# Half of the low parts of the block inputs subtracted by GpSimd, in six matmul stages of a hybrid decoder block

## The chip, the cores and the metric

The kernel runs on one core of a Trainium2 chip. The metric is the device time of one execution in microseconds (us); lower is better. Engines are called by the profile's names: PE is TensorE (PEld its weight loads), DVE is VectorE, ACT is ScalarE, POOL is GpSimd, SP is SyncE, which issues most loads.

## The reference

One decoder block over 2048 tokens of width 1024, in float32:

```python
u = rmsnorm(h, norm_mix_g); z = u @ w_in            # 1024 -> q, k, v, pz, ga, gp
a = dilated window attention(q, k, v); p = multi-scale pooling(pz)
merged = sigmoid(ga) * (a @ w_att_out) + sigmoid(gp) * (p @ w_pool_out)
h = h + merged @ w_out
m = rmsnorm(h, norm_mlp_g)
h = h + square(relu(m @ w_mlp_in)) @ w_mlp_out
return rmsnorm(h, norm_final_g)
```

## The kernel before

**Products.** A float32 product is made of three matmuls in a rounded type. `split` (L138 to L145) makes two tiles of a source tile of 128 x 512: `hi`, the rounded copy, cast by ACT (L143), and `lo` = source minus `hi`, subtracted by DVE (L144). `mm_acc` then issues three matmuls for each pair of blocks: hi times hi (L150), lo of one with hi of the other (L151), and hi with lo (L152).

**Stages.** The big projections run in a scheme of the Strassen kind: a 2 x 2 block product takes seven combined products. `stage` walks over pairs of rows of the weight, two pairs at a time; in each of the seven steps of `ORDER1` it splits the weight's combination (tiles `wh`, `wl`) and multiplies it with the input's combination (tiles `mB11h`/`mB11l`, `mT1h`/`mT1l` and so on, four tiles k = 0 to 3 each). The seven input combinations are made once for a stage, by `make` in `combine`, during its first two pairs: B11, T1, T2, B22, T3, B21, T4. The T ones are subtractions done in place (L203, L207, L212, L217): T1 overwrites the buffer that B11 was split from, T2 that of T1. So the next subtraction on a buffer has to wait until the split has read it. All input tiles stay until the stage ends.

There are six such stages: the mixer projections of the first and of the second half of the tokens (tiles with `u`; with buffer numbers `u0`, `u1`), the output projection of either half (`o0`, `o1`), and the first MLP product of either half (`c0`, `c1`). Below they are called A to F in this order. The second MLP product (L699 on) has its own splits (`xh`, `xl`) and is not touched.

**Order.** The program is put in order by a scheduler that lists instructions by its own timeline; each engine then runs its list strictly in order, waiting on semaphores. POOL's list holds no arithmetic in the stages: it issues the DMAs that write results to DRAM (`sg_d`, `mg_d`, `h_d`, `hg_d`, `hid_d`, `w2s_d`). Raw weights (`r_c` and the like) come in by SP into four buffers, so a load waits until the last use of the buffer. `w2_sums` (L691) makes the sums s1 to s4 of a second weight as a hook between pairs, out of the same four raw buffers.

Of the kernel before, what the change touches and what calls it, by code (L numbers as in the profile page):

```python
# [9 lines left out]
F32 = mybir.dt.float32  # L10
# [37 lines left out]
def trunk_kernel(ctx: ExitStack, tc, xt, w_qk, w_v, w_pz, w_grp, w_gates, w_att, w_pool, w_o, w_1, w_2, cols, out):  # L48
    nc = tc.nc
# [68 lines left out]
    def pool_of(stack, name, **kw):  # L118
        return stack.enter_context(tc.tile_pool(name=name, bufs=1, reuse_waits="tile", **kw))
# [15 lines left out]
        nc.vector.tensor_scalar(t, t, -0.5, 1.5, op0=ALU.mult, op1=ALU.add)  # L135
        nc.vector.tensor_mul(dst, y, t)

    def split(pool, src, key, tag, bufs):  # L138

        n = src.shape[-1]  # L140
        hi = pool.tile([P, C], F32R, name=f"{tag}h_{key}", tag=tag + "h", bufs=bufs)[:, :n]
        lo = pool.tile([P, C], F32R, name=f"{tag}l_{key}", tag=tag + "l", bufs=bufs)[:, :n]
        nc.scalar.copy(hi, src)  # L143
        nc.vector.tensor_sub(lo, src, hi.bitcast(F32))  # L144
        return hi, lo  # L145

    def mm_acc(ps, terms, start, stop):
# [25 lines left out]
    KH = KD // 2  # L173
    wps = ExitStack()
    wp = pool_of(wps, "wp")
# [14 lines left out]
    def combine(piece, key):  # L190


        b11, b12, b22, b21 = ({} for _ in range(4))

        def make(name):
            out = []
            for k in range(KH):
                if name == "B11":
                    x = b11[k] = piece(k, 0, "tt")
                elif name == "T1":  # L200
                    b12[k] = piece(k, 1, "hx")
                    x = b11[k]
                    nc.vector.tensor_sub(x, b12[k], x)  # L203
                elif name == "T2":
                    b22[k] = piece(k + KH, 1, "h22")
                    x = b11[k]
                    nc.vector.tensor_sub(x, b22[k], x)  # L207
                elif name == "B22":
                    x = b22[k]
                elif name == "T3":  # L210
                    x = b22[k]
                    nc.vector.tensor_sub(x, x, b12[k])  # L212
                elif name == "B21":
                    x = b21[k] = piece(k + KH, 0, "hx")
                else:
                    x = b11[k]
                    nc.vector.tensor_sub(x, b21[k], x)  # L217
                out.append(split(wp, x, f"{key}_{k}", "m" + name, KH))
            return out
        return make  # L220

# [76 lines left out]
    def stage(pairs, make, hook=None):  # L298
# [4 lines left out]
        for j0 in range(0, len(pairs), 2):  # L303
# [6 lines left out]
            for n, step in enumerate(ORDER1):  # L310
                a, b, bk = step.split()
                if j0 == 0:
                    m[b] = make(b)
                for key, _, scale, onto, fin in js:
                    wh, wl = split(wp, w[key][a], f"{key}_{a}", "w", WB)
                    first = n in (0, 1, 5)
                    if first:
                        bank[key, bk] = bank_of(bk, f"{key}_{bk}{n}")
                    ps = bank[key, bk]
                    mm_acc(ps, [(wh[:, k * P:(k + 1) * P], wl[:, k * P:(k + 1) * P], *m[b][k])  # L320
                                for k in range(KH)], first, True)
                    if n in (0, 1, 2):
                        row, t = ((0, 0), (1, 1), (0, 1))[n]
                        x = mid[key, n] = wtile(f"z{a}_{key}")
                        if onto:
                            nc.sync.dma_start(x, onto(row, t))
                            nc.vector.tensor_add(x, ps, x)
                        else:
                            total(x, ps, None, scale and scale[row])
                    elif n < 6:  # L330
                        fin(*{3: (0, 1), 4: (1, 1), 5: (0, 0)}[n], ps, mid[key, {3: 2, 4: 1, 5: 0}[n]])
                    else:
                        fin(1, 0, ps, None)
# [230 lines left out]
    def merge(hf):  # L564
# [4 lines left out]
        for t in range(2):  # L569
            c = 2 * hf + t  # L570
            for n in range(6):
                x = temp(f"p_{c}_{n}", "hx")
                nc.sync.dma_start(x, p_d[c, n])
                pa[t, n] = split(wp, x, f"pa_{c}_{n}", next(tags), KH)
# [315 lines left out]
```

## Time and profile before

| | |
|---|---|
| median of 3 runs | 2850.49 us (2848.96 to 2852.53) |
| the profiled execution, its own time | 2848.74 us |
| span of its instructions | 2847.0 us |
| PE busy | 2639.0 us, 93% |
| DVE busy | 1817.7 us, 64% |
| ACT busy | 1365.9 us, 48% |
| POOL busy | 581.7 us, 20% |
| mean granted PE clock | 0.958 |

PE is the engine that is busy nearly all the time; what counts is where it is not. Shares over the whole span are means over stages that differ much, so the rows below are taken by stretches.

### The profile page before, as it was taken

Reading aid. Unit: us, or ns where it says so; the run is one execution under the profiler, and the core shown is the slowest. Engines: PE = TensorE matmul, PEld = TensorE weight load, DVE = VectorE, ACT = ScalarE, POOL = GpSimd, SP = SyncE. Lnnn points to the kernel's source line nnn. Section 1 sums busy time; section 2 is a strip of 40 time slices with the busy share of each in tenths; the row PEclk is TensorE's granted clock in tenths of the full one; section 3 lists DMA queues with packets and bytes.
Section 4 is the critical chain, followed back from the end, with each engine's and each line's share of the span. In section 5 each row is a group of like instructions: output and inputs, shape, how many; then the busy total and the mean of one; then the engine's idle time right before and its main releaser. Section 6 shows DMA issues by size and latency. Waiting matters only on the chain.

```text
span 2847.0 us, 35963 instructions
## 1 busy us (share of the span) xinstructions
PE 2639.0 (93%) x11866; PEld 2079.0 (73%) x11866; DVE 1817.7 (64%) x3009; ACT 1365.9 (48%) x2659; POOL 581.7 (20%) x1003
## 2 busy tenths in 40 slices
PE   6999999899989996778888999989998999999996
PEld 5777777677757774556676888878887788878885
DVE  4745546854645565857888656766555585688457
ACT  5444444544444443233555555655555544564444
POOL 2134421124453342221121221122211000000000
PEclk8999999899979998898999999999999999999998
DMA  6334444244344347797675554455546746673434
GB/s 187 126 101 136 136 130 139 94 113 137 129 136 136 122 162 172 232 248 230 220 252 214 192 184 173 155 176 192 183 166 244 257 146 187 228 234 113 136 101 129
DMA packets 204650, 480.29 MB, mean 169 GB/s; under 512 B 41440, under 2 KB 44992, under 8 KB 204464
## 3 DMA queue, kind: packets, MB, share of 16 engines
q1 hardware_dynamic: 131984, 290.07, 31.8%
q0 software_dynamic: 72480, 187.93, 20.2%
q8 instruction: 94, 1.54, 0.2%
q14 instruction: 92, 0.75, 0.1%
HBM read 326.65 MB, written 151.14 MB: 168 GB/s over the span
## 4 chain that ended last, share of the span: by engine, by line
PE 72%; DMA 9%; DVE 8%; issue 7%; ACT 2%; POOL 2%; SPq 0%; DVEq 0%; POOLq 0%; ACTq 0%
PE z L152 7%; PE z L151 7%; PE z L150 6%; PE z_c_b L150 4%; PE z_c_b L152 4%; PE z_c_b L151 4%; PE z_c_c L152 3%; PE z_c_c L150 3%; PE z_c_c L151 3%; PE s L441 2%; PE z_g_b L150 2%; PE z_g_b L152 2%; PE z_g_b L151 2%; PE o L457 1%; PE z_g_c L151 1%
## 5 line engine op out<-in xcount | busy, mean ns | idle before, releaser
L144 DVE TENSOR_TENSOR wl_S<-r_S,wh_S 128x512 fp32r<-128x512 f32 x128 | 88.5, 692 | 123.6 <-ACT wh_S L143 123.6
L143 ACT CAST wh_S<-r_S 128x512 fp32r<-128x512 f32 x128 | 79.8, 624 | 175.6 <-PE z L151 157.4
L144 DVE TENSOR_TENSOR wl_c_S<-s_c,wh_c_S 128x512 fp32r<-128x512 f32 x128 | 87.9, 689 | 100.8 <-ACT wh_c_S L143 100.6
L151 PE MATMUL z<-xl_T,wh_S 128*128 128x512 f32 x384 | 149.6, 390 | 2.8 <-DVE xl_T L144 2.8
L152 PE MATMUL z<-xh_T,wl_S 128*128 128x512 f32 x384 | 149.4, 389 | 0.0
L150 PE MATMUL z<-xh_T,wh_S 128*128 128x512 f32 x384 | 138.7, 389 | 0.0
L760 POOL TENSOR_TENSOR y<-y,frs 128x256 f32<-128x256 f32 x4 | 3.2, 813 | 659.8 <-ACT fsq L745 652.2
L447 ACT ACTIVATE sb<-sb,negm 128x256 f32<-128x256 f32 (+1 forms) x192 | 87.3, 456 | 102.5 <-DVE negm L445 102.4
L143 ACT CAST wh_c_S<-s_c 128x512 fp32r<-128x512 f32 x128 | 77.6, 619 | 102.9 <-PE z_c_b L151 49.2
L443 DVE SCALAR_TENSOR_TENSOR sb<-steps,s 128x256 f32<-128x256 f32 (+1 forms) x192 | 63.7, 360 | 97.5 <-PE s L441 97.0
L144 DVE TENSOR_TENSOR wl_A<-r_A,wh_A 128x512 fp32r<-128x512 f32 x96 | 66.0, 689 | 67.3 <-ACT wh_A L143 51.1
L696 POOL DMA_DIRECT2D w2s_d<-s_w x64 | 34.6, 541 | 359.9 <-DVE s_w L275 326.1
L143 ACT CAST wh_A<-r_A 128x512 fp32r<-128x512 f32 x96 | 59.4, 620 | 101.7 <-PE z L151 76.2
L151 PE MATMUL z<-xl_B,wh_A 128*128 128x512 f32 x256 | 101.8, 398 | 3.8 <-DVE xl_B L144 3.7
L150 PE MATMUL z<-xh_B,wh_A 128*128 128x512 f32 x256 | 95.1, 404 | 6.8 <-ACT xh_B L143 6.8
L152 PE MATMUL z<-xh_B,wl_A 128*128 128x512 f32 x256 | 99.2, 396 | 0.4 <-DVE wl_A L144 0.4
L143 ACT CAST wh_c_A<-r_c 128x512 fp32r<-128x512 f32 x96 | 59.5, 620 | 60.7 <-PE z_c_c L151 31.0
L151 PEld LDWEIGHTS z<-xl_T,wh_S 128*128 128x128 f32 x384 | 72.1, 188 | 18.6 <-DVE xl_T L144 3.7
L144 DVE TENSOR_TENSOR wl_g_S<-s_g,wh_g_S 128x512 fp32r<-128x512 f32 x64 | 44.2, 690 | 64.3 <-ACT wh_g_S L143 62.4
L150 PEld LDWEIGHTS z<-xh_T,wh_S 128*128 128x128 f32 x384 | 72.1, 188 | 14.9
L152 PEld LDWEIGHTS z<-xh_T,wl_S 128*128 128x128 f32 x384 | 72.1, 188 | 14.9
L430 POOL DMA_DIRECT2D v<-v_d x96 | 61.9, 644 | 101.2 <-ACT qko L459 66.0
(665 smaller groups left out, 8687.0 us busy)
## 6 DMA issues: line engine op xcount, KB each, us to landing
x<-hid_d SPq DMA_DIRECT2D x160, 256.0 KB, 4.6
r_c<-in_w SPq DMA_DIRECT2D x64, 512.0 KB, 6.1
r_S<-w2s_d SPq DMA_DIRECT2D x128, 256.0 KB, 2.6
r_A<-in_w SPq DMA_DIRECT2D x96, 256.0 KB, 3.6
r_g<-in_w_gates SPq DMA_DIRECT2D x32, 512.0 KB, 4.2
r_w<-in_w SPq DMA_DIRECT2D x32, 512.0 KB, 3.2
w2s_d<-s_w POOLq DMA_DIRECT2D x64, 256.0 KB, 4.8
hid_d<-zS_c POOLq DMA_DIRECT2D x64, 256.0 KB, 3.7
```

Of the source, the lines that this page charges most:

```text
L143: nc.scalar.copy(hi, src)
L144: nc.vector.tensor_sub(lo, src, hi.bitcast(F32))
L150: nc.tensor.matmul(ps, lh, rh, start=start and i == 0, stop=False, skip_group_check=True)
L151: nc.tensor.matmul(ps, lh, rl, start=False, stop=False, skip_group_check=True)
L152: nc.tensor.matmul(ps, ll, rh, start=False, stop=stop and i == n - 1, skip_group_check=True)
L430: nc.gpsimd.dma_start(v, v_d[g].rearrange("(i r) f -> r i f", r=d)[r, ks, hp * P:(hp + 1) * P] .rearrange("(b p) f -> p b f", p=P))
L441: nc.tensor.matmul(ps_s[par], q[rows], k[rows], start=True, stop=True)
L443: nc.vector.scalar_tensor_tensor(s[:, par], steps[:, 2 * P - W:], SLOPES[HPG * g + 2 * hp + par] * d, ps_s[par], op0=ALU.mult, op1=ALU.add)
L447: nc.scalar.activation(s[:, par], s[:, par], AF.Exp, bias=nm[:, par:par + 1], accum_out=ls[:, par:par + 1])
L457: nc.tensor.matmul(ps_o[par * HD:(par + 1) * HD, :], v[:, b, par * HD:(par + 1) * HD], pt[:, par, b * P:(b + 1) * P], start=(b == 0), stop ...
L696: nc.gpsimd.dma_start(w2s_d[i][j], s)
L760: nc.gpsimd.tensor_mul(y, y, rs)
```

## The change

`split` gets a parameter for the engine of the subtraction, and `make` passes GpSimd for the odd k. Of 28 low parts per stage, 14 go from DVE to POOL: 84 instructions in the six stages. The casts, the weights' splits and the splits outside `make` stay as they are.

```diff
-    def split(pool, src, key, tag, bufs):
+    def split(pool, src, key, tag, bufs, lo_on=None):
...
         nc.scalar.copy(hi, src)
-        nc.vector.tensor_sub(lo, src, hi.bitcast(F32))
+        (lo_on or nc.vector).tensor_sub(lo, src, hi.bitcast(F32))
         return hi, lo
...
-                out.append(split(wp, x, f"{key}_{k}", "m" + name, KH))
+                out.append(split(wp, x, f"{key}_{k}", "m" + name, KH, nc.gpsimd if k % 2 else None))
```

The scheduler puts the whole program in order anew. Three places show what comes of it. First DVE in stage A, where the first matmuls with T1 need `mT1l_u0_0` (the number behind `u0` is k; rows with - stood there before, rows with + stand there now):

```order
 L144 TENSOR_TENSOR mB22l_u0_0_624<-xh22_0_4_1_211,mB22h_u0_0_623 128x512
-L144 TENSOR_TENSOR mB22l_u0_1_628<-xh22_0_5_1_216,mB22h_u0_1_627 128x512
 L144 TENSOR_TENSOR mB22l_u0_2_632<-xh22_0_6_1_221,mB22h_u0_2_631 128x512
-L144 TENSOR_TENSOR mB22l_u0_3_636<-xh22_0_7_1_226,mB22h_u0_3_635 128x512
 L144 TENSOR_TENSOR mT1l_u0_0_504<-xtt_0_0_0_150,mT1h_u0_0_503 128x512
 L278 TENSOR_TENSOR s3_qk0_1_1_437<-r_qk0_1_1_0_431,r_qk0_1_1_1_433 128x512
-L144 TENSOR_TENSOR mT1l_u0_1_510<-xtt_0_1_0_155,mT1h_u0_1_509 128x512
 L144 TENSOR_TENSOR mT1l_u0_2_516<-xtt_0_2_0_160,mT1h_u0_2_515 128x512
-L144 TENSOR_TENSOR mT1l_u0_3_522<-xtt_0_3_0_165,mT1h_u0_3_521 128x512
+L207 TENSOR_TENSOR xtt_0_1_0_155<-xh22_0_5_1_216,xtt_0_1_0_155 128x512
+L207 TENSOR_TENSOR xtt_0_3_0_165<-xh22_0_7_1_226,xtt_0_3_0_165 128x512
```

Two low parts are gone ahead of `mT1l_u0_0`, and two behind it; the in-place subtractions of L207 on the buffers of k = 1 and 3 stand close behind, and these buffers are now read by POOL.

Next DVE at the end of the input splits of stage F, around the sums of `w2_sums` (`s4_w2_7`, `s3_w2_7` are the last readers of two raw buffers; `s1_c1_0` belongs to the stage's first weights):

```order
-L144 TENSOR_TENSOR mB21l_c1_3_16150<-hx_c1_7_0_16147,mB21h_c1_3_16149 128x512
-L144 TENSOR_TENSOR mT4l_c1_0_16201<-tt_c1_0_0_15817,mT4h_c1_0_16200 128x512
 L686 TENSOR_TENSOR zS2_c0_14_15587<-zS2_c0_14_15587,zA11_c0_14_15512 128x512
-L144 TENSOR_TENSOR mT4l_c1_1_16206<-tt_c1_1_0_15823,mT4h_c1_1_16205 128x512
-L144 TENSOR_TENSOR mT4l_c1_2_16211<-tt_c1_2_0_15829,mT4h_c1_2_16210 128x512
-L144 TENSOR_TENSOR mT4l_c1_3_16216<-tt_c1_3_0_15835,mT4h_c1_3_16215 128x512
 L277 TENSOR_TENSOR s4_w2_7_15784<-r_w2_7_1_15779,s2_w2_7_15782 128x512
 L278 TENSOR_TENSOR s3_w2_7_15783<-r_w2_7_0_15777 128x512
 L275 TENSOR_TENSOR s1_c1_0_15797<-r_c1_0_1_15795 128x512
+L144 TENSOR_TENSOR mT4l_c1_0_16201<-tt_c1_0_0_15817,mT4h_c1_0_16200 128x512
+L144 TENSOR_TENSOR mT4l_c1_2_16211<-tt_c1_2_0_15829,mT4h_c1_2_16210 128x512
```

Besides the moved ones, the two remaining `mT4l` have gone behind the sums, so these stand sixteen places nearer to the stage's first split than before.

Last POOL in stage F, between two DMAs that write the stage before (`hid_d`):

```order
 L662 DMA hid_d0_1_82<-zc_c0_13_15451 128x512
+L144 TENSOR_TENSOR mB11l_c1_1_15826<-tt_c1_1_0_15823,mB11h_c1_1_15825 128x512
+L144 TENSOR_TENSOR mB11l_c1_3_15838<-tt_c1_3_0_15835,mB11h_c1_3_15837 128x512
+L144 TENSOR_TENSOR mT1l_c1_1_15890<-tt_c1_1_0_15823,mT1h_c1_1_15889 128x512
+L144 TENSOR_TENSOR mT1l_c1_3_15904<-tt_c1_3_0_15835,mT1h_c1_3_15903 128x512
+L144 TENSOR_TENSOR mT2l_c1_1_15956<-tt_c1_1_0_15823,mT2h_c1_1_15955 128x512
+L144 TENSOR_TENSOR mT2l_c1_3_15970<-tt_c1_3_0_15835,mT2h_c1_3_15969 128x512
+L144 TENSOR_TENSOR mB22l_c1_1_16014<-h22_c1_5_1_15952,mB22h_c1_1_16013 128x512
+L144 TENSOR_TENSOR mB22l_c1_3_16022<-h22_c1_7_1_15966,mB22h_c1_3_16021 128x512
+L144 TENSOR_TENSOR mT3l_c1_1_16070<-h22_c1_5_1_15952,mT3h_c1_1_16069 128x512
 L662 DMA hid_d0_2_83<-zS1_c0_14_15550 128x512
```

Nine of the fourteen stand in one run between two writes; the other five stand singly among the writes that follow.

## Rows read from the trace of the kernel before

**Rows 1.** Busy time by stretch: stages A to F, and one between stage starts.

```profile
core 0: us, PE busy (x) PEld busy (x) DVE busy (x) ACT busy (x) POOL busy (x), PEclk, DMA share, GB/s
52.00:74.00 22.00, 11.69 (x41) 8.24 (x40) 21.93 (x36) 10.90 (x21) 2.91 (x4) 0.77 0.12 37
505.00:562.00 57.00, 50.45 (x205) 40.42 (x204) 51.80 (x85) 28.69 (x51) 4.31 (x8) 0.90 0.28 92
1343.00:1392.00 49.00, 39.19 (x159) 30.14 (x158) 46.62 (x78) 24.22 (x44) 3.15 (x6) 0.93 0.60 186
1411.00:1465.00 54.00, 43.51 (x177) 34.36 (x176) 53.62 (x90) 33.74 (x61) 10.22 (x19) 0.91 0.70 238
1503.00:1558.00 55.00, 43.10 (x178) 33.47 (x178) 52.70 (x89) 33.26 (x61) 9.17 (x17) 0.94 0.63 227
1820.00:1870.00 50.00, 40.45 (x169) 32.60 (x169) 47.38 (x79) 35.30 (x66) 8.06 (x15) 0.92 0.50 165
1600.00:1800.00 200.00, 200.00 (x884) 165.51 (x883) 118.14 (x185) 109.17 (x188) 37.59 (x70) 1.00 0.48 171
```

**Rows 2.** Waits of PE in stages A, B, D, E, F: us, times, longest.

```profile
PE z_qk_c L151 <- DVE mT1l_u L144: 4.1, 1, 4.1
...
PE z_qk_b L150 <- ACT wh_qk_S L143: 3.5, 1, 3.5
...
PE z_o_c L150 <- ACT wh_o_S L143: 4.7, 1, 4.7
...
PE z_c_c L152 <- DVE wl_c_S L144: 5.3, 2, 3.5
...
PE z_c_b L150 <- ACT wh_c_A L143: 7.5, 1, 7.5
```

**Rows 3.** Timeline of stage F: start, us, instruction, [idle before].

```profile
1823.82 1.89 DVE L144 TENSOR_TENSOR mB11l_c<-tt_c,mB11h_c 128x512 fp32r<-128x512 f32 x3
1825.62 0.68 DVE L203 TENSOR_TENSOR tt_c<-hx_c,tt_c 128x512 f32<-128x512 f32 x1
...
1862.91 0.70 DVE L277 TENSOR_TENSOR s_w<-r_w,s_w 128x512 f32<-128x512 f32 x1
...
1863.65 0.93 SPq L285 DMA_DIRECT2D r_c<-in_w  x2
...
1868.58 0.62 ACT L143 CAST wh_c_A<-r_c 128x512 fp32r<-128x512 f32 x1 [6.17 <-DMA r_c<-in_w]
...
1869.25 0.79 PE L150 MATMUL z_c_b<-mB11h_c,wh_c_A 128*128 128x512 f32 x1 [7.46 <-ACT wh_c_A L143]
```

**Rows 4.** Timeline of stage E's end, DVE.

```profile
1554.64 0.69 DVE L640 TENSOR_TENSOR zc_o<-z_o_b,zc_o 128x512 f32<-128x512 f32 x1 [2.31 <-DMA zc_o<-in_xt]
```

**Rows 5.** POOL's only subtract-like instructions, at the kernel's end: tile view.

```profile
L760 POOL TENSOR_TENSOR y<-y,frs x4: 723/812/906, 2828.6 to 2838.4; 128x256 f32<-128x256 f32 x4
```

**Rows 6.** Timeline there, POOL and DVE, two places.

```profile
2828.58 1.59 POOL L760 TENSOR_TENSOR y<-y,frs 128x256 f32<-128x256 f32 x2 [652.23 <-ACT fsq L745]
2828.60 1.85 DVE L762 SCALAR_TENSOR_TENSOR y<-y,colt,frs 128x256 f32<-128x256 f32 x2
2830.37 0.87 DVE L762 SCALAR_TENSOR_TENSOR y<-y,colt,frs 128x256 f32<-128x256 f32 x2
...
2837.69 1.05 DVE L762 SCALAR_TENSOR_TENSOR y<-y,colt,frs 128x256 f32<-128x256 f32 x1
2837.74 1.59 POOL L760 TENSOR_TENSOR y<-y,frs 128x256 f32<-128x256 f32 x2 [7.57 <-DVE frs L136]
2838.66 1.73 DVE L762 SCALAR_TENSOR_TENSOR y<-y,colt,frs 128x256 f32<-128x256 f32 x3
```

**Rows 7.** The same DVE instruction over both places: min/median/max ns.

```profile
L762 DVE SCALAR_TENSOR_TENSOR y<-y,colt,frs x12: 472/472/1049, 2828.6 to 2840.7; 128x256 f32<-128x256 f32 x12
```

**Rows 8.** Stage F, the last input split on DVE and its first use on PE.

```profile
1861.11 1.91 DVE L144 TENSOR_TENSOR mT4l_c<-tt_c,mT4h_c 128x512 fp32r<-128x512 f32 x3
...
1902.29 0.39 PE L151 MATMUL z_c_b<-mT4l_c,wh_c_A 128*128 128x512 f32 x1
```

## The prediction

> **What bounds the kernel now.** I read the busy times by stretch first [rows 1]. Between stage starts PE has no gap: from 1600 to 1800 us it is busy for 200.00 of 200.00, while DVE is busy for 118.14. There DVE has 40% to spare, and nothing that DVE gains or loses is seen in the time. At the six stage starts it is the other way round: DVE is busy for 21.93 of 22, 51.80 of 57, 46.62 of 49, 53.62 of 54, 52.70 of 55 and 47.38 of 50 us, and PE stands for 10.3, 6.6, 9.8, 10.5, 11.9 and 9.6 us, 58.7 us together. All 84 moved instructions lie in these stretches. So the change works on the one place where DVE sets the end, and what it does to DVE's list there goes to the time nearly one to one, in either direction, since PE has no slack later to give it back.
>
> The waits of PE say what it stands for [rows 2]. In stage A it is a low part of the input itself, `mT1l` (4.1 us). In B, D, E and F it is the weights, `wh` and `wl`, not the input's parts. The timeline of F shows why [rows 3]: DVE works through its list at 0.60 us an instruction (three `mB11l` from 1823.82, the next instruction at 1825.62), reaches the sum L277 only at 1862.91, the raw buffer of the weights is then free, the load is issued at 1863.65, ACT casts at 1868.58, and PE goes on at 1869.25 after 7.46 us. The input's low parts are early by far: the last `mT4l` pieces are made around 1862 and the first is used at 1902.29 [rows 8]. So in D, E and F it does not matter when a low part is ready; it matters how late DVE gets to the weights' sums that stand behind them in its list. In stage E a load of `zc_o` ends last for a while too (2.31 us) [rows 4].
>
> **What the change removes from DVE.** I count, in the program's order, DVE's instructions from the stage's first input split up to the one that PE waits for. Stage A, to `mT1l` of k = 0: 26 before, 22 now. B, from the first B22 split to the second weight's s2: 47 and 42. C, from the first B11 split to `mT1l` of k = 2: 35 and 31. D, to the second weight's s2: 85 and 67. E, the same: 83 and 67. F, to L277: 66 and 50. That is 4 + 5 + 4 + 18 + 16 + 16 = 63 fewer; in D to F two to four more than the fourteen moved ones went behind the gate. At 0.60 us [rows 3] this takes 37.8 us off.
>
> **What it adds.** The trace has no such instruction of 512 columns on POOL. The nearest is the product at the kernel's end, 128 x 256 with two inputs in SBUF: 0.72 to 0.91 us [rows 5]. For 512 columns I bound it by 0.72 (no growth) and 1.45 us (twice 0.723). For the time of POOL itself this is harmless: fourteen are at most 20 us in a start of some 40 to 55, in which POOL is now busy for 3 to 10 [rows 1].
>
> What costs is what POOL's instruction does to DVE. At the kernel's end both run side by side twice [rows 6]. Undisturbed, DVE's L762 takes 0.47 us and starts every 0.40 (two in 0.87). Beside two POOL products, the first two take from 2828.60 to 2830.37, 1.77 us in place of 0.80: 0.97 lost. At the second place the first takes until 2838.66, 0.97 in place of 0.40, and the next three 1.73 in place of 1.27: 1.03 lost. The longest is 1049 ns against a median of 472 [rows 7]. So two POOL instructions of 256 columns cost DVE 1.0 us, 0.50 each. L762 reads two tiles from SBUF; so do nearly all DVE instructions of a stage start.
>
> The Trainium skill has a rule for this ("SBUF — State Buffer", Who interferes with whom): a VectorE instruction with two SBUF inputs and a GpSimd instruction that reads SBUF share one port pair, an exclusive lock for the whole instruction, and the second to come is blocked. The trace agrees that they exclude each other, but the loss of 0.97 and 1.03 us is smaller than the two POOL spans of 1.59 us; by the rule's "whole instruction" the upper bound below would be the price.
>
> Bounds of the price for 512 columns: 0.50 us if it did not grow with the columns, 1.45 if DVE lost all of POOL's longest time. I take 1.0, since what is lost is the time in which data are read, and that doubles. DVE instructions that read one input from PSUM were not seen beside POOL; 35 of the 279 counted above are such, and I leave an eighth of the price out for them. In the program's order 4, 8, 5, 14, 14 and 13 POOL subtractions fall before the gate of A to F: 58. They cost 58 x 1.0 x 0.875 = 50.8 us.
>
> **The sum.** 50.8 - 37.8 = 13.0 us more. On the profiled execution's own 2848.74 us this is 2861.7; that execution is 1.75 us under the median of the runs, so against the median 2850.49 + 13.0 = 2863.5 us. Costed at nothing: the moved low parts themselves (early by 40 us in F [rows 8]), the casts, which stay, and POOL's DMA issues, which have POOL's idle time around them. If that cover fails it is a rival below.
>
> The Trainium skill also says ("GPSIMD Engine Reference", Performance versus the Vector engine) that a two-input add of 2048 columns takes GpSimd 4497 ns, 1.96 times VectorE's time; an estimate from it for 512 columns is 1.1 us and some overhead, inside my bounds.
>
> **Rivals.** *Faster: the two engines hardly hinder each other here.* Then only the 37.8 us off DVE count; PE's gaps of D, E and F (10.5, 11.9, 9.6 us) are about what is taken off there (10.8, 9.6, 9.6), so the time would be near 2813, and half a price gives 2838. The point from which it decides is 37.8 / (58 x 0.875) = 0.74 us per POOL instruction. For it: instructions are longer and the alternation may leave DVE more room than at the end; against it: rows 6, which show 1.0 per 512 columns at both places. Chance 0.20.
>
> *No change.* A price near 0.74, or POOL falling behind, so that several subtractions come after the gate, when DVE no longer sets the end. 2850 within 5.7 us (0.2%, about what a measurement of this kernel can tell from no change). Chance 0.16.
>
> *Slower for another reason: what waits for POOL.* The in-place subtractions on the buffers of k = 1 and 3 wait for POOL's read, and DVE's list waits behind them; in A they stand two places behind `mT1l`. And writes in POOL's list stand behind subtractions, so that result buffers come free later by a POOL instruction or two, 1.5 to 3 us; loads like `zc_o` then come late. Two to three us in each of four stages are 10 more: 2874. For it: [rows 4]; against it: the fourteen take less than half of POOL's time. Chance 0.14.
>
> *Slower by the whole lock.* A price of 1.45 us gives 58 x 1.45 x 0.875 - 37.8 = 35.8: 2886. Rows 6 speak against it, as the loss is two thirds of POOL's span there. Chance 0.05.
>
> **How the numbers follow.** The forecast has 0.45: a price between 0.85 and 1.15 us, 2856 to 2871. The range takes in the bounds of the price: 0.50 gives 58 x 0.50 x 0.875 - 37.8 = -12.4, 2838, and 1.45 gives 2886. It leaves out the larger gains of the first rival (0.14) and a little above. Slower is 0.45 + 0.14 + 0.05 = 0.64, same 0.16, faster 0.20.
>
> **What would show it.** In the changed kernel's profile: POOL subtractions of 512 columns at 1.2 to 1.8 us, as they wait for DVE too; DVE's instructions beside them at 1.5 us or so in place of 0.69, and DVE's busy time in the starts of D to F not lower than now, although 14 instructions are gone from each; PE's gap in F longer than 7.5 us and L277 later by 1 to 2 us counted from the stage's first split; no change between stage starts. Wrong if DVE's instructions keep 0.69 us beside POOL's: then the gaps of D to F nearly close. Wrong in size if POOL's list runs behind DVE's by several steps, or if DVE is seen waiting for POOL at L203 to L217.

## The result, and the profile of the changed kernel

The changed kernel takes 2886.36 us (median of 4 runs, 2880.04 to 2891.42) against 2849.72 us before (4 runs): a ratio of 1.0129, 95% interval 1.0117 to 1.0140. It is slower by 37 us, in the direction of the forecast and nearly three times its 13 us; the end of the range (2886) is missed by a hair. The profiled execution has a span of 2884.3 us, 37.3 more than that of before, and its own numbers are used below.

The page, its span and its busy times:

```profile
span 2884.3 us, 36064 instructions
...
PE 2658.4 (92%) x11866; PEld 2085.8 (72%) x11866; DVE 1849.2 (64%) x2925; ACT 1366.4 (47%) x2659; POOL 729.0 (25%) x1087
```

DVE has 84 instructions fewer (3009 before) and is busy 31.5 us longer. At 0.60 us each, 84 are 50.4 us; so something has put 81.9 us back on DVE, 0.98 for each POOL subtraction.

Busy time by stretch, the same view as [rows 1]: the starts of stages A to F, and one stretch between them:

```profile
core 0: us, PE busy (x) PEld busy (x) DVE busy (x) ACT busy (x) POOL busy (x), PEclk, DMA share, GB/s
53.00:77.00 24.00, 11.86 (x44) 8.05 (x43) 20.29 (x28) 9.90 (x19) 19.16 (x10) 0.75 0.11 33
515.00:582.00 67.00, 56.70 (x223) 45.02 (x222) 60.40 (x77) 29.35 (x53) 27.86 (x22) 0.87 0.26 87
1358.00:1411.00 53.00, 41.85 (x150) 30.58 (x149) 49.88 (x63) 25.10 (x45) 25.80 (x21) 0.84 0.57 182
1430.00:1492.00 62.00, 48.51 (x187) 35.67 (x185) 61.49 (x78) 32.72 (x59) 30.67 (x29) 0.94 0.62 208
1530.00:1593.00 63.00, 49.98 (x190) 37.81 (x189) 61.49 (x79) 34.85 (x64) 34.83 (x32) 0.90 0.58 198
1858.00:1909.00 51.00, 37.78 (x153) 28.16 (x152) 50.86 (x61) 32.76 (x61) 28.94 (x28) 0.96 0.42 141
1640.00:1840.00 200.00, 200.00 (x883) 165.36 (x882) 119.07 (x187) 110.21 (x189) 37.62 (x70) 1.00 0.49 177
```

DVE fills the starts of D, E and F as before (61.49 of 62, 61.49 of 63, 50.86 of 51 us), though with fewer instructions. Between the starts PE is busy for 200.00 of 200.00, as forecast.

Stage F's timeline, the rows that answer to [rows 3]:

```profile
1858.21 1.80 POOL L144 TENSOR_TENSOR mB11l_c<-tt_c,mB11h_c 128x512 fp32r<-128x512 f32 x1 [1.80 <-ACT mB11h_c L143]
...
1858.78 3.50 DVE L144 TENSOR_TENSOR mB11l_c<-tt_c,mB11h_c 128x512 fp32r<-128x512 f32 x2
...
1860.25 1.48 POOL L144 TENSOR_TENSOR mB11l_c<-tt_c,mB11h_c 128x512 fp32r<-128x512 f32 x1 [0.23 <-ACT mB11h_c L143]
...
1901.71 0.68 DVE L277 TENSOR_TENSOR s_w<-r_w,s_w 128x512 f32<-128x512 f32 x1
...
1902.42 0.93 SPq L285 DMA_DIRECT2D r_c<-in_w  x2
...
1906.89 0.62 ACT L143 CAST wh_c_A<-r_c 128x512 fp32r<-128x512 f32 x1 [4.02 <-DMA r_c<-in_w]
...
1907.56 0.79 PE L150 MATMUL z_c_b<-mB11h_c,wh_c_A 128*128 128x512 f32 x1 [8.18 <-ACT wh_c_A L143]
```

Two DVE splits beside two POOL splits take 3.50 us where three took 1.89. L277 comes 42.93 us after DVE's first split of the stage (39.09 before), and PE stands 8.18 us (7.46).

One thing was not foreseen. In stage A a POOL subtraction takes 8.33 us. The tile view (min/median/max ns), and the timeline of that place, rows of POOL and DVE:

```profile
L144 POOL TENSOR_TENSOR mB22l_u<-xh,mB22h_u x4: 1251/2135/8334, 65.1 to 530.6; 128x512 fp32r<-128x512 f32 x4
```

```profile
65.13 9.55 POOL L144 TENSOR_TENSOR mB22l_u<-xh,mB22h_u 128x512 fp32r<-128x512 f32 x2 [4.66 <-ACT mB22h_u L143]
65.63 1.89 DVE L203 TENSOR_TENSOR xtt<-xhx,xtt 128x512 f32<-128x512 f32 x3
...
67.44 0.68 DVE L144 TENSOR_TENSOR wl_qk_S<-s_qk,wh_qk_S 128x512 fp32r<-128x512 f32 x1
68.04 0.68 DVE L203 TENSOR_TENSOR xtt<-xhx,xtt 128x512 f32<-128x512 f32 x1
68.64 0.68 DVE L144 TENSOR_TENSOR wl_qk_S<-s_qk,wh_qk_S 128x512 fp32r<-128x512 f32 x1
...
69.25 1.28 DVE L144 TENSOR_TENSOR mB22l_u<-xh,mB22h_u 128x512 fp32r<-128x512 f32 x2
70.45 0.68 DVE L144 TENSOR_TENSOR mT1l_u<-xtt,mT1h_u 128x512 fp32r<-128x512 f32 x1
71.05 0.68 DVE L278 TENSOR_TENSOR s_qk<-r_qk,r_qk 128x512 f32<-128x512 f32 x1
...
71.65 0.68 DVE L144 TENSOR_TENSOR mT1l_u<-xtt,mT1h_u 128x512 fp32r<-128x512 f32 x1
...
74.65 2.50 POOL L144 TENSOR_TENSOR mT1l_u<-xtt,mT1h_u 128x512 fp32r<-128x512 f32 x2
75.94 2.37 DVE L207 TENSOR_TENSOR xtt<-xh,xtt 128x512 f32<-128x512 f32 x2 [3.60 <-POOL mT1l_u L144]
```

POOL's first row holds two subtractions. The first begins at 65.13 and ends only when DVE's run of eleven instructions (65.63 to 72.33), each with two SBUF inputs and one every 0.60 us, is over; the second takes 1.25 us. During that run it is DVE that keeps 0.68 us and POOL that stands. Then DVE stands 3.60 us at L207, since POOL has not yet read the T1 buffer; the forecast had named DVE waiting for POOL at L203 to L217 as a sign that it is wrong in size.

### The profile page after: what moved, and what is told of

It is laid out like the page before. It is cut to its first block, busy times and chain, and to the rows that moved or that the text cites. A ratio compares the mean times of both kernels' runs of the same rounds, so it can differ in the third digit from the quotient of the medians.

```text
span 2884.3 us, 36064 instructions
## 1 busy us (share of the span) xinstructions
PE 2658.4 (92%) x11866; PEld 2085.8 (72%) x11866; DVE 1849.2 (64%) x2925; ACT 1366.4 (47%) x2659; POOL 729.0 (25%) x1087
## 4 chain that ended last, share of the span: by engine, by line
PE 71%; DVE 9%; DMA 8%; issue 7%; POOL 2%; ACT 2%; SPq 0%; DVEq 0%; POOLq 0%; ACTq 0%
PE z L151 6%; PE z L152 6%; PE z L150 6%; PE z_c_b L150 4%; PE z_c_b L152 4%; PE z_c_b L151 4%; PE z_c_c L151 3%; PE z_c_c L150 3%; PE z_c_c L152 3%; PE s L441 2%; PE z_g_b L150 2%; PE z_g_b L152 2%; PE z_g_b L151 2%; DMA wb<-wts_d 2%; DMA x<-hid_d 2%
## 5 line engine op out<-in xcount | busy, mean ns | idle before, releaser
L144 DVE TENSOR_TENSOR wl_S<-r_S,wh_S 128x512 fp32r<-128x512 f32 x128 | 88.3, 690 | 123.7 <-ACT wh_S L143 123.7
L144 DVE TENSOR_TENSOR wl_c_S<-s_c,wh_c_S 128x512 fp32r<-128x512 f32 x128 | 89.8, 706 | 105.5 <-ACT wh_c_S L143 105.3
L144 DVE TENSOR_TENSOR wl_A<-r_A,wh_A 128x512 fp32r<-128x512 f32 x96 | 66.1, 689 | 67.5 <-ACT wh_A L143 54.8
L144 DVE TENSOR_TENSOR wl_g_S<-s_g,wh_g_S 128x512 fp32r<-128x512 f32 x64 | 44.8, 700 | 63.9 <-ACT wh_g_S L143 59.8
L460 POOL DMA_DIRECT2D o_d<-qko x96 | 53.1, 553 | 127.4 <-ACT qko L459 124.3
```

What stands on the lines that cost most here:

```text
L144: (lo_on or nc.vector).tensor_sub(lo, src, hi.bitcast(F32))
L460: nc.gpsimd.dma_start(o_d[g][hp, :, r, own], o)
```

## The experiments

**Theory 1**: each POOL subtraction costs DVE about 1 us, more than the 0.60 it takes off, wherever it stands. **Theory 2**: the engines hinder each other little; the loss comes of what waits for POOL's list, and of the new program order.

*e1, left out.* In `make`, for odd k:

```diff
+                if k % 2:
+                    hi = wp.tile([P, C], F32R, name=f"m{name}h_{key}_{k}", tag="m" + name + "h", bufs=KH)
+                    nc.scalar.copy(hi, x)
+                    out.append((hi, out[-1][1]))
```

> The low parts of odd k are left out altogether (the low part of k - 1 is used in their place), on both engines. This gives the worth of the 84 subtractions to DVE without any price on POOL's side. Theory 1 (each POOL subtraction costs DVE about 1.0 us and gives it 0.60 back): 84 x 0.60 = 50 us off DVE, of which PE's gaps at the stage starts (58.7 us) can give back some 25 to 45: 2805 to 2825 us. Theory 2 (the new order of the program or what waits for POOL costs the time, not the engines' hindrance): DVE's relief is worth little, above 2835 us.

2814.5 us, ratio 0.9879 (0.9864 to 0.9894): 34 us less. Theory 1's number. DVE's busy time falls to 1768.8, by 48.9.

*e2, POOL writes only.* In `split`, where `lo_on` is given:

```diff
+            lo_on.memset(lo.bitcast(F32), 0.0)
```

> The odd low parts are made by POOL as in the change, but by writing zeros, with no input read (84 subtractions are left out). POOL stands in the same places with an instruction that does not read. Theory 1 (hindrance by reads): DVE's instructions keep 0.69 us, no POOL instruction waits for several us, and the time is that of the kernel with the low parts left out within 6 us, 2805 to 2830. Theory 2 (order, and waits for POOL's list): 2860 us or more.

2817.5 us, ratio 0.9890 (0.9875 to 0.9905), within 3 us of e1. The tile view of one input tile, POOL's and DVE's half:

```profile
L147 POOL MEMSET mT2l_c<- x4: 527/528/532, 1498.9 to 1816.7; 128x512 f32 x4
L145 DVE TENSOR_TENSOR mT2l_c<-tt_c,mT2h_c x4: 679/680/683, 1504.4 to 1818.5; 128x512 fp32r<-128x512 f32 x4
```

A POOL instruction that reads nothing hinders none of DVE's two-input subtractions and additions: every one that overlaps a memset takes 0.55 to 0.70 us, where one that meets a POOL subtraction in the changed kernel often takes 1.78. So what costs is in the main POOL's reading, and theory 2 falls as the main cause. Two things are not held fixed. The memset is also shorter than the subtraction (0.53 us for 1.25), which shortens all waits for POOL; and the scheduler made another order of this program too. The Trainium skill ("SBUF — State Buffer", Who interferes with whom) says that a two-input VectorE instruction contends with a GpSimd instruction that reads SBUF, and not with one that only writes; e2 beside the changed kernel agrees with both halves (at most 0.70 us beside a write, 1.78 beside a read).

One DVE instruction did pay in e2. The memsets wait for no data, so in stage A twelve run in a row, and the one-input L135 beside them, 0.42 us in the kernel before, lasts 6.22 us:

```profile
55.66 6.22 DVE L135 TENSOR_SCALAR t_x<-t_x 128x512 f32<-128x512 f32 x1
...
55.91 1.01 POOL L147 MEMSET mB22l_u<- 128x512 f32 x2
```

That is about what DVE is busy longer than in e1 (1774.0 for 1768.8 us), and stage A takes 5.4 us longer than there.

*e3, both engines.* DVE makes all low parts, POOL the odd ones once more:

```diff
         nc.vector.tensor_sub(lo, src, hi.bitcast(F32))
+        if lo_on is not None:
+            lo_on.tensor_sub(lo, src, hi.bitcast(F32))
```

> DVE makes all 28 low parts of a stage as before, and POOL makes the 14 odd ones once more into the same tiles. The cost of POOL's instructions by itself, nothing taken off DVE. Theory 1: 84 x 0.97 us = 81 us on the time of before, less what hides: 2915 to 2935 us. Theory 2: the waits for POOL are those of the change, about 2880 to 2890 us.

2915.0 us, ratio 1.0236 (1.0221 to 1.0251), 66.6 us more, at the low end of theory 1's range. DVE is busy 1884.2, 66.5 us more than before, so here DVE's loss and the time agree. It is 0.79 us for each POOL subtraction, less than the 0.98 of the change. The price alone (66.6) and the relief alone (33.9) give +32.7; the change itself has +36.6.

*e4, all but A.* `nc.gpsimd if k % 2 and key != "u0" else None`.

> The change in stages B to F alone; stage A keeps all its subtractions on DVE. Stage A lost 10.6 us in the changed kernel, beside a POOL subtraction that took 8.33 us. If that loss belongs to stage A's own POOL subtractions: 2874 to 2878 us. If it came from the start of the program or is spread otherwise: 2883 or more.

2870.4 us, ratio 1.0086 (1.0067 to 1.0105): 16 below the changed kernel, 4 below the expected window. In its trace stage A is 1.7 us shorter than before, where the change has it 8.2 us longer: that loss belongs to stage A's own subtractions.

*e5, A alone.* The same with `key == "u0"`.

> The change in stage A alone. The changed kernel and the one without stage A differ by 16 us in their medians, and stage A's own stretch grew by 8 to 11 us in the changed kernel. If stage A's loss is its own: 2858 to 2866 us, with one POOL subtraction of several us in it. If it is there only together with the rest: 2850 us within 4.

2853.4 us, ratio 1.0001 (0.9988 to 1.0014): no change, the second answer. But the trace has the loss in stage A: from A's first product to the first product with `mT4h` of the second group of pairs it takes 8.0 us longer than before. Then 5.9 us are given back between the second mixer half and the first output projection, where nothing was changed. So e4 and e5 do not add up to the change (22 + 2 against 37), and the answer's condition, a loss only together with the rest, does not hold.

*e9, a control for the order.* Before, with four one-column DVE instructions behind stage A's T1 subtractions:

```diff
                     nc.vector.tensor_sub(x, b12[k], x)
+                    if key == "u0":
+                        nc.vector.tensor_reduce(x[:, 0:1], x[:, 0:1], axis=AX.X, op=ALU.add)
```

> The kernel of before, all low parts on DVE, with four DVE instructions of one column behind stage A's in-place T1 subtractions (they write the column's own value back). They cost about 0.3 us by themselves; what else changes is the program's order. All kernels of the study with another order were 0.5 to 5.8 us faster than before in the stretch from the second mixer half to the first output projection, where nothing was changed. If that comes of the order: a time within 6 us of before, and that stretch shorter by 2 us or more. If order is worth nothing: that stretch within 1 us.

2844.95 us, ratio 0.9982 (0.9972 to 0.9993). A kernel with 0.3 us of added work is 5 to 6 us faster (by the ratio and by the medians), and the stretch without any change is 2.7 us shorter; stage C, also unchanged, is 3.3 us shorter. A new order by itself moves the time by several us, here downwards; differences of 5 us between two of these kernels say nothing of the engines.

*e6 and e11, letting POOL in.* Stage A alone, with the one-column instruction of e9 behind the T1 subtractions (e6), or ahead of them, on the column of `b12[k]` (e11).

> As the change in stage A alone, and behind each in-place T1 subtraction of stage A a DVE instruction of one column with one input (it writes the column's own value back). Theory (POOL waits as long as DVE runs instructions with two SBUF inputs back to back, and gets in beside one that needs no second input): the longest POOL subtraction of stage A is under 3 us where it was 8.33, DVE no longer stands 3.6 us at L207, and the time is 2 to 6 us below that of stage A alone. Rival (the long POOL subtraction waits for its data or for something of its own): it stays over 6 us, and the time is that of stage A alone within 2 us.

> The change in stage A alone, and ahead of each in-place T1 subtraction a DVE instruction of one column with one input; in the program's order they stand where POOL's long subtraction asks for its data (behind the eight normalizing products), not six instructions later as in the first try. Theory (POOL gets in beside a DVE instruction that needs no second input): the subtraction that took 8.33 us takes under 3 us, and DVE does not stand for it at the T2 subtractions. Rival: it takes 6 us or more again. The time is within 5 us of that of stage A alone either way.

e6: 2854.1 us (ratio 1.0002, 0.9990 to 1.0015), and the long subtraction still takes 6.53 us: a miss. The added instructions had been put at 71.69 us, late in DVE's run, and POOL got in there. e11: 2853.5 us (1.0012, 1.0003 to 1.0022). Its timeline, POOL and DVE at the place:

```profile
65.02 3.38 POOL L144 TENSOR_TENSOR mB22l_u<-xh,mB22h_u 128x512 fp32r<-128x512 f32 x2 [4.65 <-ACT mB22h_u L143]
65.52 0.27 DVE L204 TENSOR_REDUCE xhx<-xhx 128x1 f32<-128x1 f32 x3
65.71 1.57 DVE L144 TENSOR_TENSOR wl_qk_S<-s_qk,wh_qk_S 128x512 fp32r<-128x512 f32 x1
67.20 0.14 DVE L204 TENSOR_REDUCE xhx<-xhx 128x1 f32<-128x1 f32 x1
67.27 1.68 DVE L144 TENSOR_TENSOR wl_qk_S<-s_qk,wh_qk_S 128x512 fp32r<-128x512 f32 x1
```

The subtraction of 8.33 us takes 1.71: POOL gets in beside the one-column instructions, which have one input, and now DVE's next two-input instructions pay, 1.57 and 1.68 in place of 0.68. The time of stage A is no better for it (7.4 us longer than before, 8.0 in e5). Whether POOL stands or DVE pays, the stage loses about the same.

*e7, POOL copies.* `lo_on.tensor_copy(lo, src)`, one input.

> POOL makes the odd low parts by copying the source, one input read in place of two (84 subtractions are left out). Theory (any POOL instruction that reads SBUF keeps DVE's two-input instructions out while it reads): DVE instructions beside it are longer by the copy's duration less some 0.2 us, and the time is 2835 to 2886 us as that duration has it. Rival (only two inputs on both sides hinder): DVE keeps 0.69 us, 2814 to 2822 us as with POOL writing only.

2835.9 us, ratio 0.9937 (0.9919 to 0.9956). DVE is busy 27.1 us longer than in e1, 0.32 for each copy (median 0.95 us). One input read hinders too, for less. The time is at the edge of the theory's window, but its price, the copy's time less 0.2 us, would have been 0.75 and not 0.32. A copy can be kept out as well: the longest took 9.38 us.

*e8, half the columns.* POOL takes columns 0 to 255 of the odd low parts, DVE the rest.

> Of each odd low part POOL subtracts 256 columns and DVE the other 256. If the price goes by columns (half of 1.0 us for half the columns): 0.5 lost and about 0.3 gained for each, 84 x 0.2 = 17 us, with what A adds 2866 to 2878 us. If it is a price for each POOL instruction whatever its length: 84 x (1.0 - 0.3) = 59 us, 2900 to 2912 us.

2875.0 us, ratio 1.0067 (1.0047 to 1.0087). The number is in the window, but not by the sum behind it: DVE is busy for only 5.3 us more than before (1823.0), while the time grows by 19 to 24 (by the ratio and by the medians), and 18.8 of the 28 us that its profiled execution loses are in D and E. See e10.

*e10, k = 3 only.* `nc.gpsimd if k == 3 else None`, 42 subtractions.

> Only the low parts of k = 3 go to POOL, 42 in place of 84. Theory (each POOL subtraction has its price on DVE): half of the change's 37 us, 14 to 24 us more than before, 2864 to 2875. Rival (the loss comes of two POOL subtractions on each other's heels, or of the long waits of POOL, which halving takes away): less than 8 us more, 2858 at most.

2871.7 us, ratio 1.0069 (1.0052 to 1.0086), again in the window, and again with DVE up by only 4.7 us (1822.4). So an even price for each subtraction did not make the number: 14.3 us of the loss are in D and E, and stage C is 1.2 us shorter than before. The rival's number is out too, but the long waits of POOL, which halving was to take away, are there: ten POOL subtractions take over 2.5 us, up to 11.25. The waits of SP and of PE late in stage D's input splits:

```profile
SPq L225 <- POOL mB21l_o L144: 6.6, 1, 6.6
```

```profile
PE z_o_b L150 <- DVE zA_o L327: 10.6, 1, 10.6
```

A POOL subtraction takes 9.93 us there (1457.43 to 1467.36). The buffer it reads is wanted by SP's next load (L225, input of the next stage), which waits 6.6 us; SP runs its list in order, so the load of `zc_o` behind it is issued late, DVE waits for `zc_o` and makes `zA_o` late, and PE stands 10.6 us. Without any POOL read the same wait is 5.2 us (e1).

## Why the forecast had the direction and not the size

Lengths between the same matmuls, in us; "price" is the change less e1, "relief" is e1:

| stretch (before) | forecast relief, price, net | measured relief, price, net |
|---|---|---|
| A, 52.1 to 139.3 | 2.4, 3.5, +1.1 | 4.0, 12.2, +8.2 |
| B, 526.3 to 613.7 | 3.0, 7.0, +4.0 | 8.0, 12.6, +4.6 |
| C, 1352.0 to 1441.0 | 2.4, 4.4, +2.0 | 3.2, 11.2, +8.0 |
| D and E, 1441.0 to 1582.9 | 20.4, 24.5, +4.1 | 1.2, 13.5, +12.3 |
| F, 1811.4 to 1902.1 | 9.6, 11.4, +1.8 | 10.4, 13.7, +3.3 |
| all else | 0 | 4.0, 5.0, +1.0 |

The rows behind it for A, and for D and E together, each before, changed and e1 (columns as above; the second number is the length):

```profile
52.15:139.27 87.12, 75.49 (x322) 60.31 (x321) 70.72 (x111) 39.05 (x72) 15.38 (x24) 0.94 0.35 108
...
54.55:149.86 95.31, 78.33 (x323) 61.41 (x321) 73.62 (x95) 38.19 (x70) 45.04 (x37) 0.91 0.30 98
...
53.69:136.77 83.08, 76.08 (x322) 61.38 (x321) 62.11 (x95) 38.17 (x70) 14.58 (x23) 0.94 0.35 113
...
1441.02:1582.89 141.87, 122.08 (x503) 97.26 (x502) 117.45 (x192) 78.88 (x139) 28.57 (x54) 0.93 0.66 234
...
1462.62:1616.80 154.18, 129.54 (x505) 101.16 (x504) 126.16 (x174) 79.25 (x139) 63.74 (x73) 0.91 0.63 216
...
1423.17:1563.84 140.67, 124.76 (x505) 99.46 (x504) 102.86 (x168) 75.94 (x134) 28.08 (x53) 0.92 0.66 234
```

Each length holds some us of the program's order: with e2 in place of e1 the price in the five starts reads 6.9, 13.1, 13.6, 14.3 and 15.9.

**What held.** The bound: all of the change is at the stage starts, 36.4 of 37.3 us. The price of one POOL subtraction: 1.0 us was taken before the eighth, 0.98 is the mean over 84; so near a hit is partly luck, since the same working gives 0.79 in e3 and 0.71 in e10. POOL's time (1.25 us undisturbed, median 1.59; 1.2 to 1.8 was said), DVE's longer instructions (1.78 for 0.69), the longer gap in F (L277 is 3.8 us later, where 1 to 2 was said). The relief as a whole, 37.8 us forecast and 33.9 by e1's median (30.9 in the profiled execution), agrees by luck: stage by stage it does not.

**The step that failed: the price was charged for 58 subtractions, seven eighths each; it falls due for all 84.** On the profiled execution the change costs 24.3 us more than the forecast's 13.0. Of these 17.4 are price (68.2 us in place of 50.8) and 6.9 are missing relief (30.9 in place of 37.8). The forecast set one gate for each stage and took the 26 POOL subtractions behind it as free. They stand before the next thing PE waits for: ten in A, nine in C, where the price is 12.2 and 11.2 us in place of 3.5 and 4.4. In A the waits of PE show it:

```profile
PE z_qk_c L151 <- POOL mT1l_u L144: 3.1, 1, 3.1
PE z_qk_c L151 <- DVE mT1l_u L144: 2.9, 1, 2.9
PE z_qk_b L152 <- DVE wl_qk_S L144: 2.8, 1, 2.8
PE z_qk_b L151 <- DVE mT2l_u L144: 2.0, 1, 2.0
```

The second is the gate, 4.1 us before [rows 2]. The other three come behind it, 8.0 us together, and the kernel before has none of them. The first is for a moved low part itself, `mT1l` of k = 1, which the forecast had costed at nothing. And the eighth left out for DVE's PSUM readers is not saved. The 22 such instructions beside POOL's (L327, L640, L673) all keep 0.68 us, but the two-input instruction behind them can pay: L144 takes 1.18 us behind an L327 at 1438 us. With 84 x 0.98 - 84 x 0.60 = 31.9 the sum on the same execution would have been 2881; as 0.98 was measured on DVE afterwards, this says only that DVE's longer busy time is most of the 37.3.

**A second step failed in D and E, and errors hid one another.** There a relief of 20.4 us was forecast and 1.2 came. Two waits of PE in e1 show what is next there:

```profile
PE z_o_b L150 <- DVE zA_o L332: 5.2, 1, 5.2
...
PE z_c_b L150 <- ACT zA_c L297: 3.6, 1, 3.6
```

With DVE's list shorter, PE waits for the result tiles behind the load of `zc_o`, of which [rows 4] had given notice. So D and E had the price without the gain. The forecast's price there (24.5) was too high by 11.0, which hid over half of the 19.2 us of missing relief; the 8.2 that are left are the largest part of the miss in any row of the table. The forecast also had no term for PE's clock: PE's busy time itself grows by 19.4 us, 15.9 of it in these five stretches, at a lower granted clock in all of them but F (last section).

**The rivals.** "Hardly hinder each other" is out by e2 against the change. The rival of waits for POOL was right in kind. In A (DVE stands 3.60 us at L207) it is part of the price and not a thing beside it: e11 takes the wait away and the stage is as long. At the end of D the change has e10's chain in small:

```profile
SPq L225 <- POOL mT4l_o L144: 4.5, 2, 3.2
```

A POOL subtraction takes 4.56 us (1481.02 to 1485.58), the load of `zc_o` behind SP's wait is issued at 1486.02, and PE stands 4.94 us for `zA_o` (until 1494.28), a wait that the kernel before does not have. As e1 has it too, without POOL, how much of it is POOL's is not shown. "The whole lock" ends at the measured time by a price of 1.45 us for 58; what the trace shows is 0.98 for 84.

**What stays open.** DVE's 31.5 us do not account for all of 37.3. The rest is within what the order moves (e9: 5 to 6 us), and waits for POOL hold some of it (PE stands 4.4 us for tiles of POOL's, none before). In e8 and e10 the time grows far more than DVE's busy time; e10's chain makes it likely that such waits are most of the loss there, but no run shows it. How price, waits and order share the 37.3 us of the change was not separated. And why POOL gets in after one DVE instruction at some places and not after eleven at others, beyond DVE's standing still and its one-input instructions, was not settled. No version here that does all the work beats the kernel before by more than the order does.

## What to carry to other kernels

Where DVE sets the pace with two-input SBUF instructions, GpSimd is no second engine for the same work: a 128 x 512 subtraction given away saved 0.60 us and cost 0.98 (0.71 to 0.94 in e3, e4, e5 and e10). Price a move by its effect on the engine left behind, for every moved instruction and not only those before the first gate, and check with one kernel that leaves the work out and one that does it twice; together they gave +32.7 of +36.6. Ask also what waits behind the relieved engine: in D and E the next bound was 1 us away.

## What the runs showed of the hardware

*A kept-out GpSimd.* While DVE starts a two-input SBUF instruction every 0.60 us, a POOL subtraction that should take 1.25 us took 8.33 (A), 11.25 (e10) and 11.79 us (e3). It got in when DVE stood or ran an addition with one input in SBUF and one in PSUM (the one-column instructions of e6 and e11 let it in too). One input is not always free: L135 took 6.22 us beside the memsets of e2, and 1.38 in place of 0.42 beside a POOL subtraction in the changed kernel. The rule of the Trainium skill (same page and section) that the shared port pair is an exclusive lock agrees with a single meeting (DVE's 0.68 us become 1.78 beside a POOL subtraction of 1.25); these runs show besides that the waiting POOL does not get its turn after DVE's instruction, but that the next of DVE's may go first, eleven times over.

*DVE can wait out two.* In stage E one DVE instruction of 0.68 us lasts through two POOL subtractions with a 0.55 us DMA issue of POOL's between them, and PE stands for the weights behind it:

```profile
1572.77 1.29 POOL L144 TENSOR_TENSOR mB21l_c<-hx_c,mB21h_c 128x512 fp32r<-128x512 f32 x1
...
1572.86 3.52 DVE L647 TENSOR_TENSOR ssq<-ssq,sq 128x512 f32<-128x512 f32 x1
...
1574.55 1.27 POOL L144 TENSOR_TENSOR mT4l_c<-tt_c,mT4h_c 128x512 fp32r<-128x512 f32 x1
...
1577.64 0.79 PE L152 MATMUL z_c_b<-mB11h_c,wl_c_A 128*128 128x512 f32 x1 [4.40 <-DVE wl_c_A L144]
```

*A gap costs twice.* Ahead of that gap and behind it, by stretch (columns as above):

```profile
1567.00:1573.00 6.00, 6.00 (x27) 4.44 (x25) 6.00 (x9) 4.64 (x10) 5.99 (x6) 1.00 0.87 325
1577.70:1581.70 4.00, 4.00 (x10) 3.13 (x11) 4.00 (x7) 0.62 (x1) 1.55 (x2) 0.50 0.96 358
```

The granted clock is 1.00 (2.4 GHz) before PE stood for 4.40 us and 0.50 (1.2 GHz) after it, 27 matmuls in 6 us against 10 in 4. Over the whole kernel PE is busy 19.4 us longer with the same 11866 matmuls, at a mean clock of 0.953 for 0.958; the forecast looked at PE's standing time alone, which grew by 17.9. So for PE the 37.3 us are 17.9 of standing and 19.4 of longer busy time. These are not to be added to DVE's loss: 31.5 and 19.4 together are more than the whole.
